# Selected-key attention without GpSimd, and modulation rows in 512-column halves

## The chip, the cores and the metric

One core of a Trainium2 chip runs the whole program. The time is device microseconds of that core, as the median of several runs. The engines are named as the profile names them: PE (TensorE matmul) with PEld (its weight loads), DVE (VectorE), ACT (ScalarE), POOL (GpSimd) and SP (SyncE, which here only issues transfers).

## What is computed

One layer of a streaming encoder on 512 tokens of 1024 channels: a modulation of the input by a conditioning vector, two mixers side by side (retention, and attention over keys that an indexer selects), a gated sum of the two, and a mixture of 16 experts. The change touches two places.

```python
# modulation: six rows of 1024 numbers from one vector c; four of them (g1, sh2, sc2, g2) are made late
mod = jax.nn.silu(c) @ w_ada[l] + b_ada[l]
sh1, sc1, g1, sh2, sc2, g2 = jnp.split(mod, 6, axis=-1)
...
# attention over the selected keys, per block of 128 queries and per head
logits = jnp.einsum('bqhd,bqkd->bqhk', qb, kg).astype(jnp.float32) * (dh ** -0.5)
bias = rel_bias[rel_bucket(sel - qpos[None, :, None])].astype(jnp.float32)
logits = logits + jnp.transpose(bias, (0, 1, 3, 2))
logits = jnp.where(valid[:, :, None, :], logits, -jnp.inf)
p = jax.nn.softmax(logits, axis=-1).astype(vg.dtype)
return jnp.einsum('bqhk,bqkd->bqhd', p, vg)
```

The kernel doesn't gather keys. It takes all keys of the causal blocks and adds a mask (0 for a selected key, -1e30 for any other) to the logits.

## The kernel before

The program is recorded first and issued later. `Program.record` (line 248) notes every instruction with the buffers that it reads and writes; `Program.run` (line 384) then orders all of them by a list scheduling with modelled costs (`cost`, line 299; `LAT`, line 152) and slots of on-chip memory that open in phases (`Tag`, line 89; `can_alloc`, line 350). Every instruction is therefore issued from line 494, and the line numbers in the profile tell nothing of the place in the source; the shapes do. Once issued, each engine runs its own list strictly in order, and an instruction that waits holds up all behind it on its engine. SP's list holds all transfers from memory and most between buffers.

The stage of the change lies between about 252 and 410 us. Three strands are interleaved in it, for `pr` = 0 to 3 (lines 1053 to 1062):

- `dsa(pr, ...)` (line 963), the attention of two heads. The heads' queries come out of PE, are split into two halves of 16 bits (ACT, then DVE) and rearranged by four transfers of 64 KB (`stack_q`). Then four blocks of 128 queries follow, against W = 128, 256, 384 and 512 keys. A block is a chain: logits on PE; eviction with scale and bias on DVE (`stt`, line 985) into a tile `t` of two heads by W; the negated maximum on DVE (line 987); the exponential with its sum on ACT, once for each head (line 989); the reciprocal on DVE; the scaling of each head's row on DVE (line 993); transposes on PE; their eviction on ACT; and the product with the values on PE. Bias and mask are added up ahead of this by POOL into a tile `bm` (line 977), one addition of two heads by W columns for each block. PSUM holds the logits of one block at a time (`tL` has one slot), and `t` has two slots.
- `ret_out(pr)` (line 1019), gates and output projection of the retention branch: 24 matmuls of 512 columns in a row, with their weights split into two 16-bit halves by ACT and DVE (`split`, line 647, 1024 columns at a time). These matmuls are the work with which PE fills the chains of the attention.
- `mod_row(pr, q)` (line 1035), a quarter of a modulation row, 256 columns, sixteen in all. 1 MB of `w_ada` is loaded, DVE multiplies eight slices by a scalar per partition and adds them up (one `tensor_scalar`, seven `scalar_tensor_tensor`), ACT makes the upper 16-bit half, POOL the lower one, and PE sums over the partitions with a column of ones as its weights, so the result stands on one partition; DVE adds the bias there, and SP stores 256 numbers into `vec_row`.

After it come the gates of the other branch and the output projection (to about 480 us), the second norm and the router (to about 555 us), the sixteen experts (to about 680 us) and the combination.

## Time and profile before

| | us |
|---|---|
| median of three runs | 729.88 |
| lowest and highest of them | 728.83, 730.78 |
| span of the profiled execution | 726.2 |
| PE busy in it | 640.7 (88%) |
| DVE busy in it | 580.5 (80%) |
| ACT busy in it | 363.2 (50%) |
| POOL busy in it | 146.1 (20%) |

The span runs from the first to the last instruction of one execution. The median of the runs is 3.7 us above it; a time read from the trace is carried to a run's time with that difference. A busy PE is not PE at its peak, since a matmul that follows late is drawn long: the windows by stage and the waits tell more than the share of the whole span.

### The profile page before, as it was taken

What the parts mean: (1) busy time and instruction counts of PE and PEld (TensorE: products, weight loads), DVE (VectorE), ACT (ScalarE), POOL (GpSimd) and SP (SyncE); (2) the same over time, 40 slices, a digit from 0 to 9 for tenths busy, and PEclk for the clock granted to TensorE, in tenths of its full rate; (3) what the DMA queues carried; (4) which work ended last, traced back from release to release, by engine and by line L of the source; (5) the groups of instructions that cost most, each with busy time, mean ns of one, the idle gap of its engine ahead of it and who ended that gap; (6) DMA issues with size and microseconds to landing.
All of it is one profiled execution on the core that took longest, in us unless ns stands there. A gap on an engine that the chain in (4) does not pass through costs nothing.

```text
span 726.2 us, 10369 instructions
## 1 busy us (share of the span) xinstructions
PE 640.7 (88%) x3689; PEld 343.2 (47%) x3689; DVE 580.5 (80%) x1104; ACT 363.2 (50%) x581; POOL 146.1 (20%) x119
## 2 busy tenths in 40 slices
PE   3699998999998989889899999997838899999943
PEld 3355465747565635444344444444425455555411
DVE  2997699999994587998898957868883689899725
ACT  5458623343254325454373244644346688899404
POOL 1001010111011142332211100023434311101733
PEclk9699999999999999999999999999958999999987
DMA  9998524272365357444968745654536899998546
GB/s 296 359 317 241 179 69 149 70 235 66 99 206 132 110 190 217 144 131 159 304 207 278 243 186 191 212 191 153 174 132 234 299 340 371 409 351 307 99 89 232
DMA packets 93481, 151.95 MB, mean 209 GB/s; under 512 B 10449, under 2 KB 67266, under 8 KB 93298
## 3 DMA queue, kind: packets, MB, share of 16 engines
q1 hardware_dynamic: 88914, 143.21, 59.5%
q0 software_dynamic: 4464, 8.04, 4.6%
q8 instruction: 30, 0.49, 0.3%
q14 instruction: 25, 0.20, 0.1%
q10 hardware_dynamic: 48, 0.00, 0.0%
HBM read 137.91 MB, written 16.81 MB: 213 GB/s over the span
## 4 chain that ended last, share of the span: by engine, by line
PE 41%; DVE 22%; DMA 16%; issue 11%; ACT 4%; POOL 4%; SPq 1%; DVEq 0%; POOLq 0%; ACTq 0%
PE banks L494 41%; DVE arena L494 22%; DMA arena<-arena 5%; ACT arena L494 4%; DMA hrow<-arena 4%; POOL arena L494 4%; DMA arena<-in_w_in 2%; DMA arena<-in_w_exp_down 1%; DMA arena<-in_w_exp_gate 1%; SPq L494 1%; DMA arena<-in_w_ada 1%; DMA arena<-in_w_ret_out 1%; DMA arena<-in_x 1%; DMA arena<-in_w_exp_up 1%; POOL hrow L494 0%
## 5 line engine op out<-in xcount | busy, mean ns | idle before, releaser
L494 PE MATMUL banks<-arena 128*128 128x512 f16 (+9 forms) x3689 | 640.7, 334 | 72.9 <-DVE arena L494 46.3
L494 PEld LDWEIGHTS <-arena 128*128 128x128 f16 x3094 | 281.9, 100 | 297.6 <-issue 44.9
L494 DVE SCALAR_TENSOR_TENSOR arena<-arena 128x1024 f16<-128x1024 f32 (+6 forms) x374 | 311.6, 860 | 45.5 <-ACT arena L494 30.0
L494 ACT ACTIVATE arena<-arena 128x1024 f16<-128x1024 f32 (+9 forms) x296 | 244.7, 863 | 192.5 <-DVE arena L494 104.7
L494 POOL TENSOR_TENSOR arena<-arena 128x512 f32<-128x512 f32 (+5 forms) x68 | 87.1, 1284 | 449.0 <-DVE arena L494 264.8
L494 ACT ACTIVATE arena<-banks 128x512 f32<-128x512 f32 (+7 forms) x178 | 98.3, 606 | 118.7 <-PE banks L494 115.0
L494 DVE SCALAR_TENSOR_TENSOR arena<-banks,arena 128x512 f32<-128x512 f32 (+9 forms) x155 | 90.5, 604 | 37.7 <-PE banks L494 24.6
L494 PEld LDWEIGHTS banks<-arena 128*128 128x128 f32 (+2 forms) x595 | 67.4, 167 | 72.0 <-DVE arena L494 44.8
L494 DVE TENSOR_TENSOR arena<-arena 128x512 f32<-128x512 f32 (+5 forms) x92 | 50.9, 565 | 7.3 <-POOL arena L494 4.2
L494 DVE TENSOR_SCALAR arena<-arena 128x256 f32<-128x256 f32 (+8 forms) x116 | 42.7, 395 | 15.4 <-DMA arena<-in_w_ada 6.4
L494 ACT ACTIVATE arena<-banks,arena 128x128 f32<-128x128 f32 (+1 forms) x48 | 23.0, 533 | 45.3 <-DVE arena L494 24.5
L494 POOL DMA_INDIRECT hrow<-arena x15 | 27.0, 1801 | 21.6 <-DVE arena L494 15.8
L494 POOL DMA_INDIRECT arena<-u2row,arena x16 | 18.9, 1184 | 53.3 <-PE banks L494 43.8
L494 DVE MAX8 arena<-arena 128x8 f32<-128x256 f32 (+3 forms) x52 | 27.6, 530 | 1.3
L494 DVE MATCH_REPLACE8 arena<-arena 128x256 f32<-128x256 f32 (+3 forms) x56 | 27.3, 488 | 0.0
L494 DVE SCALAR_TENSOR_TENSOR arena<-arena,banks 128x512 f32<-128x512 f32 x17 | 11.7, 685 | 7.2 <-PE banks L494 7.2
L494 DVE TENSOR_REDUCE arena<-arena 128x1 f32<-128x4 f32 (+5 forms) x28 | 14.9, 532 | 0.1
L494 POOL MEMSET arena<- 128x2048 f16 (+2 forms) x12 | 11.2, 967 | 8.0 <-DMA hrow<-arena 5.3
L494 DVE TENSOR_TENSOR arena<-banks,arena 128x256 f16<-128x256 f32 x16 | 6.8, 424 | 5.6 <-ACT arena L494 5.6
L494 ACT ACTIVATION_READ_ACCUMULATOR arena<-arena 128x1 f32 x56 | 10.6, 189 | 0.0
L494 DVE TENSOR_TENSOR arena<-arena,banks 128x512 f32<-128x512 f32 (+1 forms) x12 | 6.0, 514 | 5.3 <-DMA arena<-hrow 5.3
L494 POOL COPY arena<-arena 1x1 f32<-1x1 f32 x1 | 0.8, 835 | 43.9 <-ACT arena L494 43.9
(17 smaller groups left out, 33.5 us busy)
## 6 DMA issues: line engine op xcount, KB each, us to landing
arena<-in_w_ada SPq DMA_DIRECT2D x16, 1024.0 KB
arena<-in_w_exp_gate SPq DMA_DIRECT2D x32, 512.0 KB
arena<-in_w_exp_up SPq DMA_DIRECT2D x32, 512.0 KB
arena<-in_w_exp_down SPq DMA_DIRECT2D x16, 1024.0 KB
arena<-in_w_in SPq DMA_DIRECT2D x14, 1024.0 KB
arena<-in_w_ada SPq DMA_DIRECT2D x4, 2048.0 KB
arena<-in_w_gate SPq DMA_DIRECT2D x8, 1024.0 KB
arena<-arena SPq DMA_DIRECT2D x112, 64.0 KB
```

Source lines behind the costliest of these rows:

```text
L494: o.call(*[self.real(x) for x in o.args], **{n: self.real(x) for n, x in o.kw.items()})
```

## The change

In the attention, POOL's addition and its tile `bm` are gone. The eviction adds the bias alone. One DVE instruction for each head, `tensor_tensor_reduce`, then adds the mask, turns the sign and gives the minimum, and the exponential is taken with the scale -1. The scaling by the reciprocal moves from DVE to ACT. In the modulation rows, a call handles 512 columns with two loads of 1 MB, so there are eight calls; the lower half is made by DVE, and the weights of the summing matmuls are 128 columns of ones, so that the result stands on all partitions, of which the first is used. The slots change with it: `tBM` is gone, `tMA` has two slots of 4 KB, one of them at the place of `tBM`, and `tMH` has 2 KB.

```diff
-    tBM = R.tag("SB", 4 * KB, (TMP + 16 * KB, 2, 2))
-    tMA = R.tag("SB", 2 * KB, (TMP + 52 * KB, 2, 2))
-    tMH = R.tag("SB", 1 * KB, (TMP + 72 * KB, 2, 2))
+    tMA = R.tag("SB", 4 * KB, (TMP + 52 * KB, 1, 2), (TMP + 16 * KB, 1, 2))
+    tMH = R.tag("SB", 2 * KB, (TMP + 72 * KB, 2, 2))
...
-            bm = T(tBM, [2, S])
-            POOL.tensor_tensor(bm[:, :, :W], bt[:, :, 384 - 128 * b:512], am[b][:, None, :].to_broadcast([128, 2, W]),
-                               op=OP.add)
...
-            stt(t[:, :, :W], p[:, :, :W], 0.125, bm[:, :, :W], OP.mult, OP.add)
+            stt(t[:, :, :W], p[:, :, :W], 0.125, bt[:, :, 384 - 128 * b:512], OP.mult, OP.add)
             sm = T(tSX, [3, 2])
-            DVE.tensor_reduce(sm[:, 0], t[:, :, :W], axis=AX.X, op=OP.max, negate=True)
             for i in range(2):
-                ACT.activation(t[:, i, :W], t[:, i, :W], AF.Exp, bias=sm[:, 0, i:i + 1], scale=1.0,
+                DVE.tensor_tensor_reduce(t[:, i, :W], t[:, i, :W], am[b], scale=-1.0, scalar=BIG, op0=OP.add, op1=OP.min,
+                                         accum_out=sm[:, 0, i:i + 1])
+            for i in range(2):
+                ACT.activation(t[:, i, :W], t[:, i, :W], AF.Exp, bias=sm[:, 0, i:i + 1], scale=-1.0,
                                accum_out=sm[:, 1, i:i + 1])
             DVE.reciprocal(sm[:, 2], sm[:, 1])
             for i in range(2):
-                DVE.tensor_scalar(t[:, i, :W], t[:, i, :W], sm[:, 2, i:i + 1], None, op0=OP.mult)
+                ACT.activation(t[:, i, :W], t[:, i, :W], AF.Copy, scale=sm[:, 2, i:i + 1])
...
-    onec = fixed([1], F16)
-    DVE.memset(onec, 1.0)
+    ones16 = fixed([128], F16)
+    DVE.memset(ones16, 1.0)
     def mod_row(v, q):
-        c0 = (2 + v) * D + q * 256
-        ra = T(tMR, [2048])
-        SP.dma_start(ra.rearrange("p (t c) -> p t c", c=256), w_ada[:, :, c0:c0 + 256])
-        acc = T(tMA, [2, 256])
-        SP.dma_start(acc[0:1, 1], A["b_ada"][:, c0:c0 + 256])
-        DVE.tensor_scalar(acc[:, 0], ra[:, 0:256], silw[:, 0:1], None, op0=OP.mult)
-        for t in range(1, 8):
-            stt(acc[:, 0], ra[:, t * 256:(t + 1) * 256], silw[:, t:t + 1], acc[:, 0], OP.mult, OP.add)
-        hl = T(tMH, [2, 256], F16)
+        c0 = (2 + v) * D + q * 512
+        acc = T(tMA, [2, 512])
+        SP.dma_start(acc[0:1, 1], A["b_ada"][:, c0:c0 + 512])
+        for u in range(2):
+            ra = T(tMR, [4, 512])
+            SP.dma_start(ra, w_ada[:, u * 4:u * 4 + 4, c0:c0 + 512])
+            for t in range(4):
+                w = silw[:, u * 4 + t:u * 4 + t + 1]
+                if u + t == 0:
+                    DVE.tensor_scalar(acc[:, 0], ra[:, t], w, None, op0=OP.mult)
+                else:
+                    stt(acc[:, 0], ra[:, t], w, acc[:, 0], OP.mult, OP.add)
+        hl = T(tMH, [2, 512], F16)
         ACT.activation(hl[:, 0], acc[:, 0], AF.Copy)
-        POOL.tensor_sub(hl[:, 1], acc[:, 0], hl[:, 0])
+        DVE.tensor_sub(hl[:, 1], acc[:, 0], hl[:, 0])
         p = T(tF, [512], F32, "mod")
         for i in range(2):
-            PE.matmul(p[0:1, :256], onec, hl[:, i], start=i == 0, stop=i == 1)
-        stt(acc[0:1, 1], p[0:1, :256], IWS, acc[0:1, 1], OP.mult, OP.add)
-        SP.dma_start(vec_row[v:v + 1, q * 256:(q + 1) * 256], acc[0:1, 1])
+            PE.matmul(p, ones16, hl[:, i], start=i == 0, stop=i == 1)
+        stt(acc[0:1, 1], p[0:1], IWS, acc[0:1, 1], OP.mult, OP.add)
+        SP.dma_start(vec_row[v:v + 1, q * 512:(q + 1) * 512], acc[0:1, 1])
...
-        for q in range(4):
+        for q in range(2):
             mod_row(pr, q)
```

Since the scheduling decides the order, the lists of all engines differ from the start of this stage on. Two places show what moved.

DVE's list of the kernel before, at the start of the fourth pair of heads: the eviction of the first block's logits (two heads by 128), its maximum, the second block's eviction and the first block's scaling, with pieces of modulation rows (shapes of 256 columns) and a gated product between them.

```order
L494 SCALAR_TENSOR_TENSOR arena<-banks,arena 128x2x128
L494 TENSOR_SCALAR arena<-arena 128x256
L494 TENSOR_REDUCE arena<-arena 128x2
L494 SCALAR_TENSOR_TENSOR arena<-arena,banks 128x512
L494 SCALAR_TENSOR_TENSOR arena<-banks,arena 128x2x256
L494 RECIPROCAL arena<-arena 128x2
L494 SCALAR_TENSOR_TENSOR arena<-arena 128x256
L494 TENSOR_SCALAR arena<-arena 128x128 x2
L494 TENSOR_REDUCE arena<-arena 128x2
```

The same place on DVE in the changed kernel (ISA with a tile is the new instruction, ISA without a source the read of its accumulator).

```order
L494 SCALAR_TENSOR_TENSOR arena<-banks,arena 128x2x128
L494 SCALAR_TENSOR_TENSOR arena<-arena 128x1024
L494 ISA arena<-arena 128x128
L494 ISA arena 128x1
L494 ISA arena<-arena 128x128
L494 ISA arena 128x1
L494 SCALAR_TENSOR_TENSOR arena<-banks,arena 128x2x256
L494 SCALAR_TENSOR_TENSOR arena<-arena,banks 128x512
L494 RECIPROCAL arena<-arena 128x2
L494 ISA arena<-arena 128x256
```

The two scalings have left DVE's list, a reduction of two heads has become two instructions with a read each, and half a weight split (1024 columns) now stands between the first block's eviction and its minimum.

ACT's list at the second pair of heads, in the kernel before: exponentials read the arena, the evictions of the transposes read the banks, 128x1024 is half a weight split.

```order
L494 ACTIVATE arena<-arena 128x128 x2
L494 ACTIVATE arena<-banks 128x128 x2
L494 ACTIVATE arena<-arena 128x256 x2
L494 ACTIVATE arena<-arena 128x1024
L494 ACTIVATE arena<-arena 128x384 x2
L494 ACTIVATE arena<-arena 128x1024
L494 ACTIVATE arena<-banks 128x256 x2
```

And in the changed kernel, where each arena shape of a block stands four times, two exponentials and two scalings.

```order
L494 ACTIVATE arena<-arena 128x128 x4
L494 ACTIVATE arena<-arena 128x256
L494 ACTIVATE arena<-banks 128x128
L494 ACTIVATE arena<-arena 128x256
L494 ACTIVATE arena<-banks 128x128
L494 ACTIVATE arena<-arena 128x256 x2
L494 ACTIVATE arena<-arena 128x384
L494 ACTIVATE arena<-banks 128x256 x2
L494 ACTIVATE arena<-arena 128x384
L494 ACTIVATE arena<-arena 128x1024
L494 ACTIVATE arena<-arena 128x384 x2
```

The scalings stand in ACT's list right behind the exponentials of their block, and half a weight split stands between the third block's exponentials and its scalings.

## Rows read from the trace of the kernel before

**Rows 1.** The page's first line.

```profile
span 726.2 us, 10369 instructions
```

**Rows 2.** Busy time by stage: stretch, PE, PEld, DVE, ACT, POOL, PE clock, DMA share, GB/s.

```profile
252.00:410.00 158.00, 144.36 (x784) 68.49 (x783) 137.28 (x246) 72.34 (x155) 41.60 (x29) 0.99 0.64 202
410.00:480.00 70.00, 69.91 (x324) 30.99 (x323) 50.32 (x67) 32.00 (x40) 2.39 (x3) 1.00 0.67 235
480.00:555.00 75.00, 54.85 (x404) 31.37 (x402) 58.59 (x181) 34.12 (x55) 30.41 (x21) 0.84 0.41 141
555.00:680.00 125.00, 122.21 (x747) 63.74 (x746) 105.72 (x121) 103.92 (x128) 25.41 (x17) 1.00 0.91 327
```

**Rows 3.** Waits of PE, 252 to 410 us: us in total, times, longest.

```profile
PE banks L494 <- DMA arena<-arena: 5.8, 3, 3.2
PE banks L494 <- DVE arena L494: 4.6, 3, 1.6
PE banks L494 <- POOL arena L494: 1.6, 3, 0.6
PE banks L494 <- ACT arena L494: 1.5, 3, 0.6
```

**Rows 4.** Groups by shape, PE, whole span: count, busy us, mean ns, idle before.

```profile
L494 PE MATMUL banks<-arena 128*128 128x256 f16 x432 | 52.6, 274 | 1.5 <-DMA arena<-arena 1.4
...
L494 PE MATMUL banks<-arena 128*1 128x256 f16 x32 | 8.2, 270 | 2.5 <-POOL arena L494 1.6 <-ACT arena L494 0.9
```

**Rows 5.** Groups by shape, DVE, 252 to 410 us.

```profile
L494 DVE SCALAR_TENSOR_TENSOR arena<-arena 128x256 f32<-128x256 f32 x97 | 51.7, 544 | 0.8
...
L494 DVE TENSOR_SCALAR arena<-arena 128x256 f32<-128x256 f32 x22 | 8.1, 387 | 2.0 <-DMA arena<-in_w_ada 2.0
L494 DVE TENSOR_SCALAR arena<-arena 128x128 f32<-128x128 f32 x8 | 7.0, 916 | 0.0
...
L494 DVE SCALAR_TENSOR_TENSOR arena<-banks,arena 1x256 f32<-1x256 f32 x13 | 5.3, 408 | 2.9 <-PE banks L494 1.6 <-issue 0.9
...
L494 DVE TENSOR_REDUCE arena<-arena 128x2 f32<-128x1024 f32 x4 | 4.8, 1204 | 0.0
...
L494 DVE TENSOR_SCALAR arena<-arena 128x512 f32<-128x512 f32 x8 | 3.9, 530 | 0.0
...
L494 DVE TENSOR_REDUCE arena<-arena 128x2 f32<-128x256 f32 x4 | 1.7, 415 | 0.0
```

**Rows 6.** Timeline of all engines, 359 to 366 us: start, duration, instruction, idle before.

```profile
360.56 4.52 POOL L494 TENSOR_TENSOR arena<-arena 128x768 f32<-128x768 f32 x2 [2.55 <-DVE arena L494]
...
362.41 0.47 DVE L494 SCALAR_TENSOR_TENSOR arena<-arena 128x256 f32<-128x256 f32 x1
362.79 2.56 DVE L494 TENSOR_SCALAR arena<-arena 128x128 f32<-128x128 f32 x2
365.21 0.14 PEld L494 LDWEIGHTS banks<-arena 128*128 128x128 f32 x1 [1.91 <-DVE arena L494]
365.21 5.01 PE L494 MATMUL banks<-arena 128*128 128x128 f32 x22 [1.52 <-DVE arena L494]
```

**Rows 7.** Groups by shape, DVE, 14 to 45 us, where POOL hardly works.

```profile
L494 DVE SCALAR_TENSOR_TENSOR arena<-arena 128x512 f32<-128x512 f32 x23 | 17.2, 750 | 0.4
...
L494 DVE TENSOR_TENSOR arena<-arena 128x512 f16<-128x512 f32 x4 | 2.7, 687 | 0.0
```

**Rows 8.** Groups by shape, ACT, 252 to 410 us.

```profile
L494 ACT ACTIVATE arena<-arena 128x1024 f16<-128x1024 f32 x24 | 24.6, 1050 | 12.3 <-DMA arena<-in_w_gate 7.5 <-DMA arena<-in_w_o 2.0 <-DVE arena L494 1.2
L494 ACT ACTIVATION_READ_ACCUMULATOR arena<-arena 128x1 f32 x32 | 6.1, 190 | 0.0
L494 ACT ACTIVATE arena<-arena 128x512 f32<-128x512 f32 x8 | 5.7, 718 | 2.8 <-DVE arena L494 2.8
...
L494 ACT ACTIVATE arena<-arena 128x128 f32<-128x128 f32 x8 | 3.2, 395 | 9.7 <-DVE arena L494 9.7
```

**Rows 9.** Timeline of SP: the load of the last modulation row.

```profile
457.95 0.33 SPq L494 DMA_DIRECT2D arena<-vec_row  x1
```

**Rows 10.** Timeline of DVE: the first instruction that uses a modulation row.

```profile
481.36 0.69 DVE L494 SCALAR_TENSOR_TENSOR arena<-banks,arena 128x512 f32<-128x512 f32 x1 [2.31 <-PE banks L494]
```

## The prediction, made before the changed kernel ran

> **What bounds the kernel now.** I read the busy time by stage first [rows 2], then who waits for whom in the stage of the change [rows 3], then durations by shape [rows 4, 5], and last a timeline where PE stood still [rows 6].
>
> By stage, PE is busy 69.9 of 70 us right after the stage of the change (410 to 480), and 122 of 125 us in the experts [rows 2]. There only less PE work would help. From 252 to 410 PE is drawn busy 144.4 of 158 us, and DVE 137.3, which is 87% [rows 2]. So two engines are nearly full, and PE's list has holes where it waits for DVE's chain. The holes that the profile names sum to 13.5 us: 5.8 for transfers between buffers (the rearranged queries), 4.6 for DVE, 1.6 for POOL, 1.5 for ACT [rows 3]. In all of them the matmuls behind the waiting one stand still too, so a hole that goes shortens the stage.
>
> What makes the holes for DVE is seen at 362 us [rows 6]: two scalings of 128 columns take 2.56 us, and they end 0.27 us after POOL's additions do (360.56 + 4.52 = 365.08). PE waits 1.52 us for them. The eight scalings of 128 columns average 0.916 us while eight of 512 columns, four times as long, average 0.530 [rows 5]: a DVE instruction of this kind is held as long as POOL works. POOL is busy 41.6 us in the stage [rows 2].
>
> Does a gain here reach the end? The next stage is full of PE work, and the router stage and the experts wait for what is ahead of them; DMA works at 0.41 in the router stage [rows 2], so weights aren't late by then. It is 0.91 in the experts, but those transfers follow as buffers come free, so they move along. The rows that the change makes are loaded at 458 us and first used at 481 [rows 9, 10]: 23 us of slack. I take the whole gain over.
>
> **The change part by part.**
>
> DVE's own load in the stage. Gone: 97 accumulations of 256 columns (51.7 us), their heads and the 256-column scalings (8.1), the scalings of the other widths (7.0 and 3.9 at the ends, 14.9 with the 384 columns between), 13 final additions (5.3), 16 reductions (4.8 to 1.7, 13.0 in all) [rows 5]: 93.0 us. New: 13 of the 16 quarters lie in the stage, that is 6.5 of 8 halves. A half is seven accumulations at 0.750, a head at 0.530, a subtraction at 0.687 [rows 5, 7] and a final addition, put at 0.69 like it: 7.2 us, 46.5 in all. The 32 new instructions aren't in the trace. As plain two-source instructions they take 0.750 at 512 columns [rows 7] and 0.47 at 256 [rows 6], so by the same step 0.61 at 384 and 0.33 at 128: 8 x 2.16 = 17.3 us. The read of their accumulator is bounded from above by ACT's, 0.190 [rows 8]: 32 x 0.190 = 6.1, and from below by nothing. Sum 64 to 70 us, so DVE falls from 137 to about 111 of 158 us. That alone isn't time; it is why I expect no hole for DVE to come back.
>
> PE's holes. The 4.6 us for DVE are three waits [rows 3], of which [rows 6] show one: scalings that POOL holds up; with POOL out of the stage they go. The 1.6 us for POOL are summing matmuls that wait for the lower half; DVE makes it now in 0.687 [rows 7] where POOL takes longer, and the hole goes. The bounds of the two are plus 6.2 and, if the same matmuls wait for ACT and DVE just as long, zero. I take 6.2, since nothing in [rows 6] but POOL stretched them.
>
> PE's own work. A summing matmul with one column of weights occupies PE for 8.2 / 32 = 0.256 us, while one of the same 256 columns on 128 columns of weights takes 52.6 / 432 = 0.122 [rows 4]. Sixteen of 512 columns at full pace, 69.91 / 324 = 0.216 [rows 2], take 3.5 us where 8.2 went: 4.7 us less. The low bound is zero, when the 0.13 us too many are the cost of the change between strands and not of the single column.
>
> The transfers. The 5.8 us for rearranged queries [rows 3] stay: in SP's list 1 MB pieces of `w_ada` still stand between the halves of these transfers. The pieces come in rows of 2 KB instead of 1 KB, and half as many stores into `vec_row`, each of which holds SP's list, are left; I take zero and bound it at 3 us both ways.
>
> ACT. It gets 32 scalings. The nearest rows are its exponentials of the same shapes, 0.718 to 0.395 [rows 8], some 18 us in all; it was busy 72.3 of 158 [rows 2], so it has room. In a block's chain a scaling on ACT is at most 0.25 us longer than the unheld one on DVE (0.718 against 0.530 or less at 512 [rows 5, 8]), and the minimum takes two instructions in a row instead of one of two heads; the second exponential waits for both, the first for one alone. What hides this is the other work in PE's list: gates and output projections stand between a block's logits and its transposes. Zero, then, with plus 4 us (16 x 0.25) as the bound against.
>
> Sum: 4.6 + 1.6 + 4.7 = 10.9 us less. The span goes from 726.2 [rows 1] to 715.3; the median of the runs lies 3.7 above the span, so 719.0.
>
> **A rule against the change.** [Rows 7] show a two-source DVE instruction at 0.750 us for 512 columns, which is full pace without an accumulator. The Trainium skill, "Vector Engine (DVE) Microarchitecture Reference", section "Points that are easy to get wrong", says of the scalar_tensor_tensor form that two 32-bit sources in the on-chip memory halve the throughput, because no port is left for the accumulator. No row shows one with an accumulator. If the new instruction counts as of that form, the second rival below holds, 727.7; by the rows alone the forecast does, 719.0.
>
> **The rivals.**
>
> *More goes than I count.* With DVE and POOL relieved, the holes for transfers and ACT close too (5.8 + 1.5 [rows 3]). That is 18.2 us less, 711.7. For it: 64-KB transfers queue behind `w_ada`, whose rows get longer. Against: their place in SP's list is the same.
>
> *The new instruction runs at half pace.* Each takes twice as long, 17.3 us more on DVE, about 1.1 us for each of 16 blocks, in the chain. DVE would still be under its old load (128 against 137), but half of it, 8.7 us, would show as holes ahead of the transposes: 719.0 + 8.7 = 727.7. For it: no row shows two sources and an accumulator at once, so nothing contradicts it. Against: DVE's single-source reductions of two heads run at 1.204 us for 1024 columns [rows 5], full pace while they reduce.
>
> *ACT becomes the late one, and the kernel is slower.* A scaling that was DVE's stands in ACT's list with half a weight split, 1.05 us [rows 8], between exponential and scaling in some blocks, and PE's transposes behind it. If every block paid one split and the longer scaling, that would be 16 x (1.05 + 0.25) = 20.8 us. From 10.9 / 1.3, that is nine blocks of sixteen on, the gain is eaten; at two thirds of the blocks it is 13.9 - 10.9 = 3 us slower, 732.9. For it: the list shows such splits at that place, and ACT's weight splits themselves wait for transfers (12.3 us idle before them [rows 8]), which then holds the scaling. Against: ACT has more than half its time free.
>
> *Nothing arrives.* The stage shortens, but router or experts take it back, by another order of their lists or a later slot for weights (one place now stays with `tMA` until the last modulation row is opened): about 729.5. Against: the slack of 23 us [rows 9, 10].
>
> **How the numbers follow.** The forecast, 719 (715 to 724), gets 0.43; more than that, 711.7, 0.12; half pace, 727.7, 0.18; ACT late, 732.9 and above, 0.19; nothing arrives 0.08. A measurement of this kernel can tell 0.3%, 2.2 us: below 727.7 is faster, above 732.1 slower. Faster: 0.43 + 0.12 and half of the half-pace case, 0.64. Same: its other half and the last case, 0.17. Slower: 0.19. The range leaves out the far half of the second case and that of the slow one: 710 to 733.
>
> **What would show it.** Right: POOL without work between 252 and 410 us; no scaling or accumulation on DVE longer than its kind; DVE near 111 to 114 busy of a stage of some 147 us; no holes of PE for DVE or POOL; summing matmuls at 0.22 us. Wrong, and how: the new instruction over 1 us at 512 columns (half pace); holes of PE for ACT of a microsecond ahead of transposes (ACT late); a stage that is 11 us shorter under a span that isn't (nothing arrives).

## The result, and the profile after

The changed kernel takes 719.69 us (median of 4 runs, 718.14 to 724.11) where the kernel before takes 730.33 beside it: a ratio of 0.986, 95% interval 0.982 to 0.990. That is 7 to 13 us faster. The forecast was 719.0. Of all runs behind the ratios below, four slow ones, more than 1.5% above the fastest of their kernel, are left out: one of eleven with the short addition, and three of twelve of the kernel before with the changed tail order.

The page of the changed kernel, its first line and the busy times (busy us, share of the span, instructions), which answer to [rows 1]:

```profile
span 718.1 us, 10181 instructions
## 1 busy us (share of the span) xinstructions
PE 638.4 (89%) x3673; PEld 345.5 (48%) x3673; DVE 552.3 (77%) x1056; ACT 375.7 (52%) x605; POOL 100.3 (14%) x87
```

Busy time by stage, which answers to [rows 2]; the stretches are moved as the work moved (columns: stretch, length, PE, PEld, DVE, ACT, POOL, PE clock, DMA share, GB/s):

```profile
252.00:396.00 144.00, 136.91 (x762) 69.08 (x760) 117.31 (x216) 86.34 (x182) 0.00 (x0) 0.99 0.72 234
396.00:466.00 70.00, 70.00 (x326) 31.67 (x325) 42.19 (x49) 29.71 (x37) 0.23 (x1) 1.00 0.57 200
466.00:541.00 75.00, 55.45 (x401) 31.02 (x400) 56.88 (x181) 33.39 (x54) 28.84 (x21) 0.82 0.40 141
541.00:670.00 129.00, 124.65 (x746) 64.55 (x745) 105.49 (x121) 104.53 (x128) 24.00 (x16) 0.99 0.89 319
```

POOL has no work in the stage of the change, and DVE is busy 117 us of 144. What PE waits for between 252 and 396 us is one row now, where [rows 3] have four (us in total, times, longest):

```profile
PE banks L494 <- DMA arena<-arena: 7.0, 3, 4.1
```

The holes for DVE, POOL and ACT, 7.7 us before, are gone; those for the rearranged queries stay, 7.0 where they were 5.8. DVE's groups by shape in this stretch, which answer to [rows 5, 7] (count, busy us, mean ns, idle before):

```profile
L494 DVE SCALAR_TENSOR_TENSOR arena<-arena 128x512 f32<-128x512 f32 x56 | 41.8, 746 | 2.5 <-DMA arena<-in_w_ada 1.7
...
L494 DVE CUSTOM_DVE_ANT_0 arena<-arena 128x512 f32<-128x512 f32 x8 | 5.2, 680 | 0.0
...
L494 DVE CUSTOM_DVE_ANT_0 arena<-arena 128x384 f32<-128x384 f32 x8 | 4.1, 553 | 0.0
...
L494 DVE CUSTOM_DVE_ANT_0 arena<-arena 128x256 f32<-128x256 f32 x8 | 3.0, 413 | 0.0
L494 DVE DVE_READ_ACCUMULATOR2_ANT arena<- 128x1 f32 x32 | 2.6, 82 | 0.0
...
L494 DVE CUSTOM_DVE_ANT_0 arena<-arena 128x128 f32<-128x128 f32 x8 | 2.0, 287 | 0.0
```

`CUSTOM_DVE_ANT_0` is the new instruction that masks and takes the minimum, and the row after its 256-column shape is the read of its accumulator. ACT's groups by shape there, which answer to [rows 8]; counts of 16 are exponentials and scalings together:

```profile
L494 ACT ACTIVATE arena<-arena 128x512 f32<-128x512 f32 x16 | 11.0, 714 | 1.2 <-DVE arena L494 1.0
...
L494 ACT ACTIVATE arena<-arena 128x128 f32<-128x128 f32 x16 | 5.9, 393 | 14.5 <-DVE arena L494 14.5
```

**Where the gain arose and where some of it went.** Two places divide the span well in all kernels. DVE's last `MAX8` of the key selection lies ahead of what the change moves (of all lists, only one POOL instruction of 0.23 us has another place before it):

```profile
195.90 0.69 DVE L494 MAX8 arena<-arena 128x8 f32<-128x512 f32 x1
```

(kernel before). The first matmul of the router, of 20 columns, starts at 499.95 us before and at 486.02 after. From the one to the other is 304.1 us before and 290.8 after, 13.3 less. From the router's first matmul to the end it is the other way round: 226.3 before, 232.1 after, 5.8 more. So by these two profiles the changed kernel wins more in its stage than it keeps.

### The profile page after: what moved, and what is told of

It reads as the page before. It is cut to its first block, busy times and chain, and to the rows that moved or that the text cites. A ratio compares the mean times of both kernels' runs of the same rounds, so it can differ in the third digit from the quotient of the medians.

```text
span 718.1 us, 10181 instructions
## 1 busy us (share of the span) xinstructions
PE 638.4 (89%) x3673; PEld 345.5 (48%) x3673; DVE 552.3 (77%) x1056; ACT 375.7 (52%) x605; POOL 100.3 (14%) x87
## 5 line engine op out<-in xcount | busy, mean ns | idle before, releaser
L494 PE MATMUL banks<-arena 128*128 128x512 f16 (+9 forms) x3673 | 638.4, 335 | 66.4 <-DVE arena L494 43.3
L494 ACT ACTIVATE arena<-arena 128x1024 f16<-128x1024 f32 (+8 forms) x320 | 258.1, 846 | 192.1 <-DVE arena L494 94.0
L494 DVE SCALAR_TENSOR_TENSOR arena<-arena 128x1024 f16<-128x1024 f32 (+7 forms) x318 | 294.0, 949 | 62.9 <-ACT arena L494 48.4
L494 PEld LDWEIGHTS banks<-arena 128*128 128x128 f32 (+2 forms) x595 | 69.3, 168 | 69.4 <-DVE arena L494 38.0
L494 POOL TENSOR_TENSOR arena<-arena 128x512 f32<-128x512 f32 (+2 forms) x36 | 41.7, 1160 | 291.5 <-DVE arena L494 237.3
L494 DVE TENSOR_TENSOR arena<-arena 128x512 f32<-128x512 f32 (+6 forms) x100 | 56.0, 571 | 9.2 <-POOL arena L494 5.8
L494 DVE TENSOR_SCALAR arena<-arena 128x1 f32<-128x1 f32 (+7 forms) x76 | 22.6, 328 | 11.8 <-ACT arena L494 5.7
L494 POOL IOTA arena<- 128x4 int32 (+2 forms) x3 | 1.5, 502 | 188.8 <-PE banks L494 188.7
L494 DVE CUSTOM_DVE_ANT_0 arena<-arena 128x128 f32<-128x128 f32 (+3 forms) x32 | 14.3, 483 | 0.0
L494 ACT ACTIVATION_READ_ACCUMULATOR arena<-arena 128x1 f32 x56 | 10.5, 188 | 0.0
L494 DVE BATCH_NORM_STATS2 arena<-banks 128x6 f32<-128x128 f32 x32 | 7.1, 285 | 3.3 <-PE banks L494 3.2
```

Source lines behind the costliest of these rows:

```text
L494: o.call(*[self.real(x) for x in o.args], **{n: self.real(x) for n, x in o.kw.items()})
```

## The experiments

Each ran beside the kernel before, on the same chip. Stage is the time from the last `MAX8` to the router's first matmul, rest from there to the end, both from the one profiled execution. Ratios come from 6 to 12 runs of each kernel (4 of the changed one) beside 16 or 17 of the kernel before (4).

| kernel | ratio to before (95%) | stage | rest |
|---|---|---|---|
| before | 1 | 304.1 | 226.3 |
| changed | 0.986 (0.982 to 0.990) | 290.8 | 232.1 |
| modulation rows alone | 0.985 (0.982 to 0.988) | 296.7 | 224.8 |
| rows alone, one column of ones | 0.982 (0.978 to 0.986) | 296.2 | 225.3 |
| attention alone | 0.991 (0.987 to 0.994) | 297.4 | 227.1 |
| before, short addition on POOL | 0.992 (0.990 to 0.995) | 299.2 | 224.6 |
| before, short sums on DVE | 0.996 (0.993 to 0.999) | 302.6 | 226.7 |
| before, 128 columns of ones | 0.996 (0.993 to 1.000) | 301.8 | 226.1 |
| changed, one column of ones | 0.988 (0.985 to 0.991) | 292.3 | 234.2 |
| changed, scalings on DVE | 0.976 (0.972 to 0.980) | 288.1 | 228.6 |
| changed, tail order | 0.980 (0.976 to 0.985) | 290.3 | 225.1 |
| changed, scalings on DVE, tail order | 0.978 (0.975 to 0.981) | 290.0 | 228.9 |
| changed, experts' order | 0.981 (0.977 to 0.985) | 292.9 | 228.3 |
| before with the changed tail order | 1.004 (1.000 to 1.008) | 301.4 | 231.5 |

Three sets show how far one execution's stage repeats, since their instructions are in the same order to just ahead of the router: 304.1 and 301.4 (before, and before with the changed tail), 290.8, 290.3 and 292.9 (changed, tail order, experts' order), 288.1 and 290.0 (scalings on DVE, without and with the tail order). That is 2.7 us at most, and differences below it are not read as effects. A single kind of wait repeats no better. The kernel before with the changed tail has the same instructions in the same order in the stage, and PE's waits for DVE, 252 to 410 us, are 6.3 us there where [rows 3] have 4.6, while all four kinds together are 13.3 and 13.5:

```profile
PE banks L502 <- DVE arena L502: 6.3, 5, 1.6
```

TensorE's clock ahead of the change differs between executions too: between 195 and 252 us the mean grant was 1.00 (2.4 GHz throughout) in the kernel before, 0.97 in the changed one (part of it at 1.2 GHz), and 0.94 with the rows alone, the changed kernel with one column, and the short sums. The kernel before and the short sums there (columns as in the windows above):

```profile
195.00:252.00 57.00, 53.27 (x343) 34.28 (x343) 41.07 (x94) 22.63 (x35) 8.38 (x6) 1.00 0.51 150
```

```profile
195.00:252.00 57.00, 53.70 (x326) 34.67 (x325) 39.74 (x89) 22.70 (x35) 7.37 (x5) 0.94 0.48 144
```

Where that matters, the way to the router is also counted from one and the same TensorE matmul at about 252 us, behind that stretch; that count repeats to 3.4 us (247.8 in the kernel before, 244.4 with the changed tail).

The gain of the stage is 13.3 us in the pair of profiles, and 11.4 between the means of the first two sets (302.7 and 291.3).

**The rows alone, and the attention alone.** The first is the kernel before with the new `mod_row`, the second with the new `dsa`:

```
-        for q in range(4):
+        for q in range(2):
             mod_row(pr, q)
```

> The kernel before with the modulation rows in 512-column halves (128 columns of ones, lower half on VectorE), and attention as before. Theory of the prediction: single-column matmuls and the wait for GpSimd's lower half go, 4.7 + 1.6 = 6.3 us of the stage, while GpSimd's mask additions and the holes for VectorE (4.6 us) stay; span 4 to 6 us under the kernel before. Rival, VectorE's load is what binds: it falls by some 17 us here, the holes for VectorE close too, and the stage gives 9 us or more. Rival, the single column costs nothing: 2 us or less.

> The kernel before with the changed attention (bias at eviction, mask and negated minimum in one instruction, scaling on ScalarE), and the modulation rows in 256-column quarters with one column of ones and GpSimd's subtraction. Theory of the prediction: the holes for VectorE (4.6 us) go, of those for GpSimd (1.6 us) a part, and the summing matmuls keep their price; the stage gives 5 to 6 us, the span 3 to 6. Rival, VectorE's load: the attention takes only some 12 us off it, the accumulations of 256 columns stay, so holes for VectorE stay and the stage gives 2 us or less. Rival, ScalarE late: new holes for ScalarE ahead of the transposes, and no gain.

The rows alone save 9 to 13 us by their ratio, as much as the whole change; the attention alone 4 to 9. By profiles the stage gives 7.4 and 6.7 us against the profile of before (6.0 and 5.3 against the mean of its two), and the rest hardly changes. The two stage gains add up to about what both give together. The rows' stage is what was expected; their 9 to 13 us in all are more than the 4 to 6 that were. With the rows alone, PE still waits for DVE as long as before, 4.3 us where it was 4.6, and POOL still holds the scalings. Waits of PE, 252 to 410 us, and DVE's 128-column scalings, rows alone:

```profile
PE banks L494 <- DMA arena<-arena: 4.5, 3, 2.3
PE banks L494 <- DVE arena L494: 4.3, 4, 1.7
```

```profile
L494 DVE TENSOR_SCALAR arena<-arena 128x128 f32<-128x128 f32 x8 | 7.6, 995 | 0.0
```

So this gain isn't POOL's hold-up. Of the 13.5 us of named waits 8.8 are left; those for POOL and ACT, 3.1, are gone. With the attention alone PE has no wait for DVE, and those for ACT grow to 3.4 us (1.5 before), which the second rival of its expectation named; still there is a gain. Waits of PE, 252 to 410 us, attention alone:

```profile
PE banks L494 <- ACT arena L494: 3.4, 3, 1.9
PE banks L494 <- DMA arena<-arena: 2.0, 1, 2.0
PE banks L494 <- POOL arena L494: 1.3, 1, 1.3
```

**POOL's additions cut short.** All engines keep the order of the kernel before. The additions are cut to one column a head, and the eviction adds the bias alone, so this run leaves the mask out of the logits.

```
-            POOL.tensor_tensor(bm[:, :, :W], bt[:, :, 384 - 128 * b:512], am[b]..., op=OP.add)
+            POOL.tensor_tensor(bm[:, :, 0:1], bt[:, :, 0:1], am[b]..., op=OP.add)
...
-            stt(t[:, :, :W], p[:, :, :W], 0.125, bm[:, :, :W], OP.mult, OP.add)
+            stt(t[:, :, :W], p[:, :, :W], 0.125, bt[:, :, 384 - 128 * b:512], OP.mult, OP.add)
```

> The kernel before in its own order on every engine, with GpSimd's mask addition cut to one column a head, and the bias added at the eviction (the mask is left out of the logits). VectorE, ScalarE and TensorE do what they did; only GpSimd's 40 us are gone. If GpSimd's additions hold VectorE up: scalings of 128 columns fall from 0.916 us to 0.3 or less, the holes for VectorE (4.6 us) go, the lower halves come earlier (1.6 us), and the stage is 4 to 6 us shorter; VectorE busy some 10 us less for the same instructions. If the holes come from VectorE's own load: scalings keep their time, and the stage changes by less than 1 us.

The eight scalings, the same instructions in the same order, fall from 0.916 us [rows 5] to 0.280. DVE's groups by shape, 252 to 410 us:

```profile
L494 DVE TENSOR_SCALAR arena<-arena 128x128 f32<-128x128 f32 x8 | 1.9, 280 | 0.0
```

That POOL's additions held DVE up is shown by this. The kernel gains 4 to 8 us by its ratio, the stage 4.9 (3.5 against the mean of the two profiles of before). But the holes that the profile puts down to DVE are mostly still there, in four places now. Waits of PE, 252 to 410 us, short addition:

```profile
PE banks L494 <- DMA arena<-arena: 4.8, 3, 2.0
PE banks L494 <- DVE arena L494: 3.3, 4, 1.3
PE banks L494 <- ACT arena L494: 0.6, 1, 0.6
PE banks L494 <- POOL arena L494: 0.5, 2, 0.3
```

4.6 us (6.3 in the repeat) became 3.3. So the size of the step was right, and its reading of the rows wrong: the holes named for DVE did not close, all four kinds became smaller, 13.5 to 9.2 in all.

**DVE's own load.** Again the order of the kernel before; only the sums of the modulation rows are narrower, and leave out 96 of each 256 columns.

```
-            stt(acc[:, 0], ra[:, t * 256:(t + 1) * 256], silw[:, t:t + 1], acc[:, 0], ...)
+            stt(acc[:, 0, :160], ra[:, t * 256:t * 256 + 160], silw[:, t:t + 1], acc[:, 0, :160], ...)
```

> The kernel before in its own order on every engine, with the 112 accumulations of the modulation rows cut from 256 to 160 columns (the other columns of the sums are left out). VectorE gets some 10 us less work, as in the run with GpSimd's short addition (11.8 us), and GpSimd, ScalarE and TensorE do what they did. If VectorE's load as such sets the stage: 4 us or more off the stage, ratio 0.994 or less, though the 128-column scalings stay at 0.9 us. If only GpSimd's hold-up at the scalings counts: 1.5 us or less, ratio 0.998 or more.

0.4 to 5 us by its ratio, with a middle of 2.8, which lies between the two expectations; the stage alone can't decide it (302.6, with the lower clock ahead of it). Counted from the same matmul at about 252 us, the way to the router is 243.8 us, where the short addition takes 243.3 and the two profiles of the kernel before 247.8 and 244.4. PE's holes for DVE are 4.2 us, all four kinds 10.0. So DVE's load counts for something. By the middles of the ratios (2.8 against 5.7 us) it counts for less than POOL's hold-up of about the same number of microseconds, but the two intervals overlap and the profiles don't tell them apart.

**One column or 128.** In the kernel before and in the changed one, and with the rows alone:

```
-    onec = fixed([1], F16)
+    ones16 = fixed([128], F16)
...
-            PE.matmul(p[0:1, :256], onec, hl[:, i], start=i == 0, stop=i == 1)
+            PE.matmul(p[:, :256], ones16, hl[:, i], start=i == 0, stop=i == 1)
```

> The kernel before with 128 columns of ones in place of one in its 32 summing matmuls, nothing else. Price at each side of a single-column matmul or pair of them (28 places, 0.19 us each): 5.3 us less work for TensorE. Price per column, as the prediction took it: 32 x 0.134 = 4.3 us. No price of its own: 0. How much of it brings the first router matmul forward is open: with one column in the changed kernel the holes for transfers between buffers took up nearly all of 2.9 us; here, if that is general, 2 us or less; if it was a matter of that order, 4 us or more.

> The changed kernel with one column of ones in the 16 summing matmuls, nearly the same order of instructions otherwise. Price per streamed column, as the prediction took it (0.256 against 0.122 us for 256 columns): 16 x 0.27 = 4.3 us more in the stage. Price per change between one column and 128 columns of weights, at each side of such a matmul (0.094 us in the starts of the kernel before: 0.309 from the start of the matmul ahead where 0.216 would do, 0.202 to the next where 0.108 would do): at most 16 x 0.19 = 3.0 us more, and the same 0.19 for 512 columns as for 256. No price of its own: 0. In the span up to a third of it may be lost on the way to the end.

> The modulation rows in halves alone, but with one column of ones. TensorE gets some 3 us of work back. If the relief of VectorE (10.6 us less busy) makes the gain of the halves, most of it stays: 6 to 10 us under the kernel before, ratio 0.986 to 0.992, and the holes for VectorE shrink as TensorE gets slower. If the single column's price makes it: 5 us or less, ratio 0.993 or more.

PE's busy time can't show the price. It goes from 640.7 to 636.2 us in the kernel before, and from 638.4 back to 641.3 in the changed one, but profiles of kernels with the same matmuls in the stage differ as much: 639.7 with the short addition and 644.7 with the short sums, 635.7 with the tail order. The starts of the matmuls show it. It is a price per change between one column and 128 columns of weights, not per streamed column. In the kernel before, the starts around a lone single-column matmul of 256 columns are 0.309 us after the matmul ahead (full pace: 0.216 for 512 columns) and 0.202 to the next (full pace 0.108). In the changed kernel with one column of ones and 512 streamed columns they are 0.310 and 0.309 (full pace 0.216): 0.094 us at each side again. With 128 columns of ones in the kernel before, the same places start at full pace, 0.216 and 0.109, so it isn't the change between strands that costs. For all places that makes 28 x 0.19 = 5.3 us of PE's work in the kernel before and 13 x 0.19 = 2.5 in the changed one.

What arrives is another matter. In the kernel before, as its PE gets faster, its holes for DVE grow from 4.6 us (6.3 in the repeat) to 7.9. Waits of PE, 252 to 410 us, before with 128 columns of ones:

```profile
PE banks L494 <- DVE arena L494: 7.9, 7, 2.0
PE banks L494 <- DMA arena<-arena: 5.2, 4, 2.4
PE banks L494 <- POOL arena L494: 1.7, 3, 0.7
PE banks L494 <- ACT arena L494: 1.7, 2, 0.9
```

16.5 us of holes where there were 13.5; the ratio gives a gain of 0 to 5 us. In the changed kernel the opposite happens: one column costs 2.5 us of PE's time, the holes for transfers are 5.0 where three profiles with 128 columns have 6.0 to 7.0, and the router starts 0.3 us later. With the rows alone the version with one column isn't slower by its ratio either (0.982 against 0.985, beyond both of its expectations), but its clock ahead of the change was higher (1.00 against 0.94): counted from the same matmul at about 252 us, it takes 242.6 us to the router, and 128 columns take 240.1. Counted so, the changed kernel takes 233.1 with one column and 233.5 to 234.7 with 128. So of some 5 us of PE's work in the kernel before, 0 to 5 are time by the ratio, and of 2.5 in the other two all or nothing; one execution of each can't tell more.

**The scalings.** The changed kernel with its 32 scalings on DVE again:

```
-                ACT.activation(t[:, i, :W], t[:, i, :W], AF.Copy, scale=sm[:, 2, i:i + 1])
+                DVE.tensor_scalar(t[:, i, :W], t[:, i, :W], sm[:, 2, i:i + 1], None, op0=OP.mult)
```

> The changed kernel with the 32 scalings back on VectorE. Theory (what stretched them was GpSimd, which has no work in the stage now): they take their unheld times there, 0.53 us at 512 columns and 0.3 or less at 128, VectorE gets some 12 us more work, no hole of TensorE for VectorE comes back, and the first router matmul stays within 2 us of the changed kernel's 486.0 us. Rival, VectorE's load was the limit: holes for VectorE of 3 us or more come back, and the router starts 3 us or more later. Rival, ScalarE is late in the changed kernel: the router starts earlier.

This is the fastest kernel of the study by its median, 713.17 us against 730.44. Its router starts 3.9 us earlier than in the changed kernel, at 482.1, where at most 2 were expected; 1.3 of them lie ahead of the stage. PE's holes for DVE are 0.2 us, so none came back. The stage is shorter by 2.6 us, within what repeats, but the rest is shorter too (228.6 against 232.1), and there the scalings do nothing. What differs there is the order in which router and experts are issued: the planner orders them by modelled times, and another stage ahead gives another order.

**The order behind the stage.** The changed kernel, with its router and experts in the order that the planner gave them in the kernel before, on PE, ACT, DVE and POOL (`TAIL` lists them by their place in the program; it lists SP's transfers too, whose order is the same in both kernels):

```
+    R.tail_from, R.tail = len(R.ops), TAIL
     def psm():
         return T(tB4, [512])
...
+        rank, turn = {}, dict.fromkeys(free, 0)
+        for e in self.tail:
+            for i, n in enumerate(self.tail[e]):
+                rank[ops[self.tail_from + n]] = i
...
                 for o in lst:
+                    if o in rank and rank[o] != turn[e]:
+                        continue
```

> The changed kernel with the router's and the experts' instructions of TensorE, ScalarE, VectorE and GpSimd held to the order that they have in the kernel before; the stage of the change and SyncE's list as they are. From the first router matmul to the end the kernel before takes 226.3 us, the changed one 232.1, each half alone 224.8 and 227.0. If the other order of these instructions is what gives the gain back: 226 to 228 again, span 712 to 714, some 5 us under the changed kernel. If the transfers of the weights give it back (the experts' stream follows its own pace): 231 to 233 and a span of 717 to 719.

> The reverse of the run with the tail order: the kernel before, with the router's and the experts' instructions of TensorE, ScalarE, VectorE and GpSimd in the order that they have in the changed kernel. If that order is what costs the changed kernel its 5.8 us behind the stage: 230 to 234 us from the first router matmul to the end instead of 226.3, and the whole 3 to 7 us slower than the kernel before (ratio 1.004 to 1.010). If the order costs only together with the earlier stage (because the weights come late by then): 225 to 228, ratio 0.998 to 1.002.

The rest is 225.1 us with the order of before and 232.1 with its own, and 231.5 in the kernel before when it takes over the changed order. By kernels: seven profiles with the order of before behind the stage (the attention alone has it too) show 224.6 to 228.9, three with the changed order 231.5 to 234.2. The ratios point the same way with less: 0.980 instead of 0.986 here, some 4 us, and 1.004 there, some 3 us; taken singly, neither is clear of the noise, since the first two intervals overlap and that of the last just includes 1. So the changed kernel loses 5 to 7 us by the pairs of profiles, and 3 to 4 by the ratios, through the order of instructions that the change doesn't touch. Parted at the first gather of the experts' tokens, all profiles with one of the two orders give (us):

| | router's first matmul to the first gather | from there to the end |
|---|---|---|
| order of before | 41.0 to 41.4 (nine profiles) | 183.5 to 187.5 (nine) |
| order of the changed kernel | 42.7 to 43.8 (five) | 188.6 to 191.4 (three) |

Two places of the loss are seen. On DVE, the fourth token tile's first half is evicted at the same moment in both, but the second half 2.2 us later in the changed kernel, after a longer wait for PE. Timeline of DVE: start, duration, instruction, idle before; the changed kernel, then the one with the tail order:

```profile
504.36 0.67 DVE L494 SCALAR_TENSOR_TENSOR arena<-banks,arena 128x512 f32<-128x512 f32 x1
504.96 0.17 DVE L494 TENSOR_REDUCE arena<-arena 128x2 f32<-128x32 f32 x1
...
512.70 0.69 DVE L494 SCALAR_TENSOR_TENSOR arena<-banks,arena 128x512 f32<-128x512 f32 x1 [2.73 <-PE banks L494]
```

```profile
504.35 0.68 DVE L502 SCALAR_TENSOR_TENSOR arena<-banks,arena 128x512 f32<-128x512 f32 x1
504.95 1.39 DVE L502 TENSOR_SCALAR arena<-arena 128x128 f16<-128x128 f32 x2
...
510.47 0.69 DVE L502 SCALAR_TENSOR_TENSOR arena<-banks,arena 128x512 f32<-128x512 f32 x1 [1.25 <-PE banks L502]
```

The first gathers follow, 2.2 us apart, though the router's first matmuls start together (486.02 and 485.93):

```profile
529.51 1.83 POOL L494 DMA_INDIRECT arena<-u2row,arena  x1 [10.31 <-DVE arena L494]
```

```profile
527.33 1.83 POOL L502 DMA_INDIRECT arena<-u2row,arena  x1 [6.97 <-DVE arena L502]
```

The other place is in the first experts, from the changed kernel's timeline of all engines:

```profile
571.62 0.33 SPq L494 DMA_DIRECT2D arena<-in_w_exp_gate  x1
...
573.53 2.00 ACT L494 ACTIVATE arena<-arena 128x1024 f16<-128x1024 f32 x2 [3.29 <-DMA arena<-in_w_exp_gate]
574.62 1.23 DVE L494 SCALAR_TENSOR_TENSOR arena<-arena 128x1024 f16<-128x1024 f32 x1 [3.12 <-ACT arena L494]
...
576.32 1.97 PE L494 MATMUL banks<-arena 128*128 128x128 f32 x8 [3.18 <-DVE arena L494]
```

ACT's list has a weight split whose transfer isn't in; DVE's half of that split stands ahead of the expert's own work on DVE, and PE waits 3.18 us. In the same stretch, 545 to 610 us, the kernel with the tail order waits 1.2 us for DVE. The wait alone is a part of the loss only, for the kernel before has one of 2.6 us there too. What differs as well is TensorE's clock behind it. Between 560 and 580 us, the changed kernel, then the kernel before (columns as in the windows above):

```profile
560.00:580.00 20.00, 16.82 (x110) 9.23 (x108) 13.30 (x15) 13.51 (x17) 5.12 (x4) 0.91 0.98 337
```

```profile
560.00:580.00 20.00, 17.37 (x99) 8.61 (x97) 12.99 (x16) 11.48 (x16) 5.73 (x3) 1.00 0.85 289
```

In all three profiles with the changed order of the experts PE waits 3.2 to 5.9 us for DVE there, and the grant then falls to 1.2 GHz for a part of the next 15 us (means of 0.89, 0.77 and 0.89). In the nine with the order of before it stays at 2.4 GHz from 555 to 675 us. A mean of 0.91 over 20 us is worth an estimated 1.8 us. In the last run the lists in `TAIL` begin with the first expert's weights, so that the router keeps the changed kernel's order:

> The changed kernel with only the experts' instructions in the order of the kernel before, the router's as in the changed kernel. In the changed kernel the part from the first router matmul to the end is 5.8 us longer than before: 2.1 up to the first gather, 3.7 behind it. If each order costs on its own, the 3.7 go and the 2.1 stay: 228 to 229 us for that part, ratio 0.981 to 0.985. If the router's order brings the experts' loss with it (its late third tile holds up the first loads): 231 or more, ratio as the changed kernel's, 0.986. If the router's order costs nothing by itself: 225 to 227.

The rest is 228.3 us, as expected if both places count by themselves: to the first gather 43.8 (the loss stays), behind it 184.4 where the changed kernel takes 188.6 and the kernel before 184.9 (the loss is gone, as far as one profile can show it).

**Both together.** Scalings on DVE, and the tail order:

> The changed kernel with the scalings back on VectorE and the router's and experts' instructions in the order of the kernel before. The two gains are taken to be independent: the stage as with the scalings back alone (some 2 us shorter than in the changed kernel), and 225 to 227 us from the first router matmul to the end. That makes 4 us less than with the scalings back alone, where this last part took 228.6: a ratio of 0.965 to 0.972 to the kernel before. If the scalings' place does nothing by itself, and their run alone was better only by its own order behind the stage: the same as the tail order alone, 0.980.

0.978, which isn't better than either alone (0.976 and 0.980). So the two are one gain, not two. The traces show why: with the scalings on DVE, the planner's own order behind the stage is, by operations and shapes on every engine, that of the last run above, the router's as in the changed kernel and the experts' as in the kernel before, and the rest is the same too (228.6 and 228.3 us). Behind equal orders, then, scalings on DVE or on ACT give 0.976 or 0.981, and 0.978 or 0.980; both pairs lean to DVE, by 2 to 4 us, and both stay within their intervals. The scalings' place does nothing that these runs could tell. By their medians all three are faster than both kernels: 15 to 21 us under the kernel before with the scalings on DVE, 11 to 18 with the tail order, 14 to 18 with both. The first and the last also have intervals below that of the changed kernel.

## Why the prediction was right, point by point

The time came out within 0.7 us of the forecast, although two of its steps failed: the summing matmuls, whose place other relief took, and the carry to the end.

**The holes for DVE and POOL, 6.2 us.** They went. That POOL's additions stretch the scalings is shown (0.916 to 0.280 us), and the price of that, 4 to 8 us in the kernel before, agrees with 4.6 + 1.6. Only the step from [rows 6] to the three holes was too direct: with POOL's hold-up alone gone, 3.3 of the 4.6 us stood in other places; with the whole attention changed, the profile names none for DVE.

**The summing matmuls, 4.7 us.** As PE's work it is near, 5.3 us by the starts, though the price is that of a change between the widths, which the prediction didn't name; its low bound, a price of the change between strands, is refuted by the starts with 128 columns of ones. As a term of the sum it isn't borne out: 0 to 5 us arrive by the ratio, with a middle of 2.6, since holes open or close behind it. The rows still gave what was put down for them (6.3 us with the wait for POOL; 6.0 to 7.4 in the stage), and their gain by the ratio, 9 to 13 us, is there with one column too. What the rows save besides, from DVE's load, was taken for "not time". The short sums put 0.4 to 5 us on a relief of that size (10.5 us less of DVE's busy time, 10.6 with the rows alone); the remainder wasn't separated from the fewer transfers and stores of the halves.

**The transfers, 5.8 us that stay.** They stayed: 6.0 to 7.0 in three profiles. The 1.5 us for ACT, which only the rival "more goes than I count" let go, went, so that part of the rival came true.

**ACT, zero.** Right: scalings on ACT or on DVE behind the same order give 0.980 and 0.978. DVE's 117 us in 144 are near the forecast of 111 to 114 in 147, but by two errors that partly cancel: all eight halves lie in this stretch (56 accumulations, seven each), not 6.5, which is 10.7 us more, and the new instructions with their reads take 16.9 us where 17.3 to 23.4 were put down.

**The new instruction.** 0.680, 0.553, 0.413 and 0.287 us against 0.750, 0.61, 0.47 and 0.33 forecast, and 0.082 for the read against a bound of 0.190: 16.9 us with the reads. It runs at the pace of the plain two-source form, and the half-pace rival is refuted. The rule that spoke for it (the Trainium skill, "Vector Engine (DVE) Microarchitecture Reference", section "Points that are easy to get wrong") doesn't carry over to this instruction, which reads two 32-bit sources from the on-chip memory and accumulates: measured, it is quicker than the two-source form without an accumulator at 0.746. The rule is stated for the `scalar_tensor_tensor` form, and no run here shows that form with an accumulator.

**The carry, the whole gain.** This step failed. The rival "nothing arrives" got 0.08 and named the mechanism, another order of the lists behind; it came true for 5 to 7 us by the profiles and 3 to 4 by the ratios, not for all. The prediction argued from waits and slack of data (23 us for the modulation rows, transfers that move along), and the order of the transfers wasn't at fault: SP's list was the same in the run that removed the loss. Nothing in the trace of before could show it. The order of the instructions could have: the router's and the experts' lists differed from those of before in places that the change doesn't touch.

**The sum.** 10.9 us was forecast for the stage and all of it for the end. The stage gave 11.4 to 13.3, the order behind it took 5 to 7 in the profiles, and the stretch ahead of the stage was 0.6 us shorter. The span was forecast at 715.3 and came out at 718.1, 8.1 us under that of before instead of 10.9. The median of the runs was put 3.7 us above the span, as before; it lies 1.6 above it, and 10.6 under the median of before, with 7 to 13 in its interval. That the end came out at 719 is in part luck: a stage that was a little too small, carried over too fully, and an offset that was too large.

## What to carry to other kernels

Where a planner orders a whole program by modelled times, compare the order behind the change as well as in it: here it cost between a quarter and a half of what the stage gained, and with the order held as it was the gain is 2.0% instead of 1.4%. Work taken off the tensor engine need not be time while another engine's chain sets the holes, and a named hole may move rather than close; ask of each term which wait grows when it goes, and profile the same order twice before a wait that moved by 2 us is read as an effect. An engine that looks only slow may be held by a neighbour: the same instruction three times as long in one stretch as in another is the sign, and cutting the neighbour's work in an unchanged order shows its price.

## What was not expected of the hardware

A matmul on one column of weights between matmuls on 128 columns costs 0.094 us at each side, with 256 or 512 streamed columns alike; two of them in a row pay it once. DVE's instruction with an accumulator over two float32 sources took 0.680 us for 512 columns, less than a two-source instruction without one (0.746), and reading its accumulator 0.082, under half of ACT's 0.190. POOL's additions stretched a 128-column scaling on DVE from 0.280 to between 0.916 and 0.995 us.
